# A decoder layer step in split float32 on one core: 30 weight subtractions moved from GpSimd to DVE

## The chip, the cores and the metric

One core of one Trainium2 chip runs the kernel. The metric is the device time of one execution in microseconds, the median over several runs. The engines are TensorE (matmuls; PE and PEld in the profile), DVE (VectorE), ScalarE (ACT), GpSimd (POOL) and SyncE (SP), which here issues most transfers. Each engine works through its own queue in order.

## The reference

One layer of a hybrid decoder, for 1024 prompt tokens and 8 x 4 sample tokens that share all weights (model width 1024). Cut to what matters here:

```python
h = x * (1 + scale1) + shift1
z = h @ w_in                       # q, k, v and the two GLU halves
mix = jnp.concatenate([attn_out, conv_out], axis=-1) @ w_out
x = layer_norm(ALPHA * x + gate1 * mix, ln1_g, ln1_b)
h = x * (1 + scale2) + shift2
up, new_ffn_buf = causal_dwconv(ffn_buf, h @ w_up, ffn_conv_w, ffn_conv_b)   # width 3
up_a, up_b = jnp.split(up, 2, axis=-1)
f = (jax.nn.silu(up_a) * up_b) @ w_down
x = layer_norm(ALPHA * x + gate2 * f, ln2_g, ln2_b)
```

`attn_out` is differential attention, `conv_out` a GLU with a causal convolution of width 31 and a LayerNorm. All arrays are float32.

## The kernel before

**Split products.** Each product of float32 matrices is made of three matmuls in the type float32r: with w = whi + wlo and x = xhi + xlo it adds whi xhi, whi xlo and wlo xhi in PSUM (`mm3`, lines 176 to 178). The high half is a cast, the low half is the float32 value less its high half.

**Tokens and chunks.** The 1056 tokens lie on the free axis in three chunks (`NCH`) of 352 columns (`CH`); the features lie on the partitions in 8 blocks of 128 (`KD`). `gemm8` makes one 128x352 output block with 24 matmuls. A weight block is 128x1024 float32, 512 KB.

**The weight pipeline.** `wsrc` lists the weight blocks in the order of their use, each with the way its low half is made. `prefetch_w` takes the next block: a load by SP into `wst` (2 buffers), a cast on ScalarE into `whi` (L159), and the low half into `wlo` (3 buffers each). The ways are "dma" (ScalarE writes the negated high half, L161, and a DMA of GpSimd's queue adds the original block, L162) or one `tensor_tensor` subtract (L164) on the engine that stands in the list. `next_w` gives out a block and looks two blocks ahead. The load's issue is L303 (`load`).

**The stage around the change.** Behind the attention comes the output projection: for each of the chunks 0, 1, 2 the loop `project` makes 8 output blocks and so takes the 8 blocks of `w_out` once per chunk, 24 in all. DVE adds each block, times its gate, to the residual `acc` (`residual`, L1179). The LayerNorm of chunk 0 is spread over the projection of chunk 1, that of chunk 1 over the projection of chunk 2, and that of chunk 2 over the first FFN group. Its steps (`norm_steps`) are on DVE: a halving sum over the 8 feature blocks (`presum`: L201, then L204 twice, in the tile `bs_s`), then a column sum by TensorE (`colsum`, L210, two for each LayerNorm), the mean taken off (L223), squares by ScalarE (L224), the halving sum again and a second column sum, the reciprocal root (`rstd`: L187 on ScalarE, L189 to L191 on DVE), and its product with the residual (L232). Then `modulate` (L284 to L295, on ScalarE and DVE) makes the high and low halves `h2h` and `h2l` of the FFN's input, and `affine` (L299, GpSimd, 8 steps per chunk) scales the residual.

The FFN works through 11 groups of two feature blocks. The first and the last group (`CHUNK_OUTER`) run their up-products chunk by chunk, and so take their 4 blocks of `w_up` three times each; with the 2 blocks of `w_down` the first group takes 14 blocks. In `Up.chunk` ScalarE takes the product out of PSUM (L1062, L1063), DVE adds the two other taps of the convolution (L1068, L1072) and multiplies the halves (L1079), and GpSimd makes the low half of the result (`al`, L1082); small fills and copies of the state are GpSimd's too (L1048, L1049, L1085, L1086). `down` adds to the residual with L1179.

**Order.** The order of instructions in each engine's queue is drawn up by a list scheduler at compile time; weight loads are kept in program order on SP in the first part of the kernel. Waits are set by the tiles that an instruction reads and writes.

Of the kernel before, what the change touches and what calls it, by code (L numbers as in the profile page):

```python
# [18 lines left out]
KD = D // 128  # L19
# [5 lines left out]
NCH = 3  # L25
# [11 lines left out]
FG = 2  # L37
# [9 lines left out]
CHUNK_OUTER = (0, KF // FG - 1)  # L47
# [21 lines left out]
def body(tc, nc, io):  # L69
    ex = ExitStack()  # L70
    with ex:
# [54 lines left out]
        wsrc = []  # L126
        for w, i in ORDER:
            wsrc += [(io["w_in"][m], "dma") for m in ((16 + i, 12 + i) if w == "g" else (4 * "qkv".index(w) + i, ))]
        wsrc += [(io["w_out"][m], nc.gpsimd) for c in range(NCH) for m in range(KD)]
        for f0 in range(0, KF, FG):  # L130
            once = nc.gpsimd if f0 // FG == CHUNK_OUTER[0] else "dma"

            def blocks(what, how):
                return [(io["w_up"][m], how) for f in range(f0, f0 + FG) for m in (f, KF + f)] if what == "u" else \
                    [(io["w_down"][f], how) for f in range(f0, f0 + FG)]

            if f0 + FG == KF:
                for w, cs in LAST:
                    if w != "n":
                        wsrc += blocks(w, "dma" if len(cs) > 1 else nc.vector)  # L140
            else:
                wsrc += blocks("u", once) * (NCH if f0 // FG in CHUNK_OUTER else 1) + blocks("d", once)
# [1142 lines left out]
```

## Time and profile before

| | us |
|---|---|
| median of 3 runs | 1448.97 |
| lowest and highest run | 1442.78, 1452.08 |
| the profiled execution | 1445.67 |
| its span, first to last instruction | 1443.9 |
| TensorE busy (matmul) | 1354.2 |
| DVE busy | 911.7 |
| ScalarE busy | 643.1 |
| GpSimd busy | 412.9 |

The busy times are of the profiled execution, and are averages over stages that differ: the stage of the change has to be looked at by itself. An instruction that has started and stands because of another engine counts as busy. The granted clock is given as a share of TensorE's full speed of 2.4 GHz, so that 0.50 is the lower level of 1.2 GHz. In the timeline the bracket behind an instruction is the time that its engine was idle before it, and what ended that.

### The profile page before, as it was taken

The page shows a single profiled execution, that of the slowest core. Times are in us where ns is not written, and L with a number is a line of the kernel's source. Part 1 is how long each engine was busy: PE and PEld are TensorE (multiplying, and loading weights), DVE is VectorE, ACT ScalarE, POOL GpSimd, SP SyncE. Part 2 cuts the span into 40 slices and gives each one's busy share as a digit, 9 for nine tenths or more (in the row PEclk, how much of TensorE's full clock was granted, in tenths as well). Part 3 has the DMA queues.
Part 4 walks back from the last instruction along what each step waited for, and adds up shares of the span by engine and source line. Part 5 has one row for each costly group of instructions (what it writes and reads, how often), then busy time and mean ns, then how long its engine had stood idle before and what let it go on. Part 6 is the DMA issues. An engine that isn't in the chain of part 4 may idle for free.

```text
span 1443.9 us, 24578 instructions
## 1 busy us (share of the span) xinstructions
PE 1354.2 (94%) x9449; PEld 1268.2 (88%) x9449; DVE 911.7 (63%) x1924; ACT 643.1 (45%) x1170; POOL 412.9 (29%) x484
## 2 busy tenths in 40 slices
PE   7899999999999898878999999999999999999993
PEld 6798999996766798777999999999999999999983
DVE  5859999427777578897454445454545454536497
ACT  6532222456666554554344343434343434352532
POOL 2431110421110588776121212222222212222111
PEclk9999999999999999989999999999999999999997
DMA  9877666548764254333252434343343434342627
GB/s 311 273 228 199 185 185 191 147 131 288 234 229 172 100 163 143 109 102 102 59 117 65 111 69 108 73 103 81 96 87 90 102 74 100 77 109 67 174 72 207
DMA packets 71670, 199.67 MB, mean 138 GB/s; under 512 B 16002, under 2 KB 16514, under 8 KB 70658
## 3 DMA queue, kind: packets, MB, share of 16 engines
q1 hardware_dynamic: 57874, 145.55, 30.2%
q0 software_dynamic: 13680, 52.57, 18.6%
q8 instruction: 74, 1.21, 0.3%
q14 instruction: 42, 0.34, 0.1%
HBM read 137.49 MB, written 15.51 MB: 106 GB/s over the span
## 4 chain that ended last, share of the span: by engine, by line
PE 70%; DMA 10%; DVE 9%; issue 4%; ACT 4%; POOL 1%; SPq 1%; DVEq 0%; POOLq 0%; ACTq 0%
PE psb L176 20%; PE psb L178 20%; PE psb L177 19%; DMA wlo<-wst 5%; PE psa L836 3%; PE psb L877 2%; DVE t L1068 2%; PE psa L319 1%; PE psb L866 1%; DVE bs_s L204 1%; PE psb L788 1%; PE psb L753 1%; DMA wada<-w_ada 1%; DMA y<-gb 1%; DMA wst<-w_in 1%
## 5 line engine op out<-in xcount | busy, mean ns | idle before, releaser
L1068 DVE SCALAR_TENSOR_TENSOR t<-up,prm,t 128x352 f32<-128x352 f32 (+1 forms) x264 | 177.8, 673 | 288.6 <-ACT t L1063 283.4
L177 PE MATMUL psb<-h2l,whi 128*128 128x352 f32 x1056 | 341.5, 324 | 6.3 <-DVE h2l L295 6.3
L176 PE MATMUL psb<-h2h,whi 128*128 128x352 f32 x1056 | 343.2, 326 | 2.4 <-ACT h2h L294 2.4
L178 PE MATMUL psb<-h2h,wlo 128*128 128x352 f32 x1056 | 339.8, 325 | 0.8 <-DMA wlo<-wst 0.8
L159 ACT CAST whi<-wst 128x1024 fp32r<-128x1024 f32 x124 | 129.2, 1050 | 323.3 <-PE psb L177 278.5
L177 PEld LDWEIGHTS psb<-h2l,whi 128*128 128x128 f32 x1056 | 201.2, 191 | 7.4 <-DVE h2l L295 6.9
L1179 DVE SCALAR_TENSOR_TENSOR acc<-psb,mod,acc 128x352 f32<-128x352 f32 (+1 forms) x288 | 160.3, 571 | 73.0 <-PE psb L178 67.0
L176 PEld LDWEIGHTS psb<-h2h,whi 128*128 128x128 f32 x1056 | 199.8, 189 | 3.0 <-ACT h2h L294 2.7
L178 PEld LDWEIGHTS psb<-h2h,wlo 128*128 128x128 f32 x1056 | 199.6, 190 | 1.9 <-DMA wlo<-wst 1.3
L176 PE MATMUL psb<-ah,whi 128*128 128x352 f32 x528 | 172.1, 328 | 6.5 <-DVE acc L1179 3.3
L178 PE MATMUL psb<-ah,wlo 128*128 128x352 f32 x528 | 166.3, 326 | 8.3 <-DMA wlo<-wst 8.3
L177 PE MATMUL psb<-al,whi 128*128 128x352 f32 x528 | 171.4, 325 | 0.0
L162 POOL DMA_DIRECT2D wlo<-wst x80 | 71.3, 892 | 347.9 <-ACT wlo L161 319.2
L178 PE MATMUL psb<-hh,wlo 128*128 128x352 f32 x480 | 156.8, 327 | 4.3 <-DMA wlo<-wst 4.3
L176 PE MATMUL psb<-hh,whi 128*128 128x352 f32 x480 | 157.8, 335 | 1.5 <-ACT sig L399 1.5
L177 PE MATMUL psb<-hl,whi 128*128 128x352 f32 x480 | 155.8, 325 | 0.0
L375 DVE SCALAR_TENSOR_TENSOR cv<-u,prm,cv 128x1024 f32<-128x1024 f32 x120 | 151.4, 1296 | 0.8
L1082 POOL TENSOR_TENSOR al<-g,ah 128x352 fp32r<-128x352 f32 x60 | 61.3, 1022 | 234.8 <-ACT ah L1080 234.8
L164 POOL TENSOR_TENSOR wlo<-wst,whi 128x1024 fp32r<-128x1024 f32 x38 | 103.5, 2729 | 32.8 <-ACT whi L159 32.7
L176 PEld LDWEIGHTS psb<-ah,whi 128*128 128x128 f32 x528 | 99.7, 189 | 11.1 <-DVE acc L1179 6.4
L178 PEld LDWEIGHTS psb<-ah,wlo 128*128 128x128 f32 x528 | 98.3, 189 | 11.2 <-DMA wlo<-wst 11.2
L177 PEld LDWEIGHTS psb<-al,whi 128*128 128x128 f32 x528 | 99.7, 189 | 0.0
(253 smaller groups left out, 2291.4 us busy)
## 6 DMA issues: line engine op xcount, KB each, us to landing
wlo<-wst POOLq DMA_DIRECT2D x80, 512.0 KB, 5.4
wst<-w_up SPq DMA_DIRECT2D x56, 512.0 KB, 3.7
wada<-w_ada SPq DMA_DIRECT2D x48, 512.0 KB, 5.5
kv<-kc SPq DMA_DIRECT2D x64, 256.0 KB, 5.4
kv<-vc SPq DMA_DIRECT2D x64, 256.0 KB, 4.7
wst<-w_out SPq DMA_DIRECT2D x24, 512.0 KB, 3.7
wst<-w_down SPq DMA_DIRECT2D x24, 512.0 KB, 4.3
wst<-w_in SPq DMA_DIRECT2D x20, 512.0 KB, 3.8
```

The costliest lines, as they stand in the source:

```text
L159: last_w["hi"] = nc.scalar.copy(hi, st)
L162: last_w["lo"] = nc.gpsimd.dma_start(lo.bitcast(F32), st, accum_op=ALU.add)
L164: last_w["lo"] = how.tensor_tensor(lo, st, hi.bitcast(F32), op=ALU.subtract)
L176: nc.tensor.matmul(ps, lhsT=wh, rhs=xh, start=start and i == 0, stop=False)
L177: nc.tensor.matmul(ps, lhsT=wh, rhs=xl, start=False, stop=False)
L178: nc.tensor.matmul(ps, lhsT=wl, rhs=xh, start=False, stop=stop and i == n - 1)
L375: nc.vector.scalar_tensor_tensor(acc, src, wj, acc, op0=ALU.mult, op1=ALU.add)
L836: nc.tensor.matmul(ps[m][:, i, :w], lhsT=q[r], rhs=k[r, i * w:(i + 1) * w], start=True, stop=True)
L877: nc.tensor.matmul(po[:, 0, :128], lhsT=at[:, (kt - k0) * 128:(kt - k0 + 1) * 128], rhs=V[:, kt, h * 128:(h + 1) * 128], start=(kt == 0), ...
L1068: nc.vector.scalar_tensor_tensor(t[:, :npc], up[:, o + j:o + j + npc], w, t[:, :npc], op0=ALU.mult, op1=ALU.add)
L1082: eng.tensor_tensor(self.al[:, c, :], g, self.ah[:, c, :].bitcast(F32), op=ALU.subtract)
L1179: nc.vector.scalar_tensor_tensor(x[:, :npc], ps[:, :npc], gate[:, 0:1], x[:, :npc], op0=ALU.mult, op1=ALU.add)
```

## The change

The subtracts of 30 weight blocks are given to DVE in place of GpSimd: those of `w_out` for chunks 1 and 2 (16), and those of the first FFN group (12 of `w_up`, 2 of `w_down`). The 8 of chunk 0 stay with GpSimd. Nothing else is edited; the scheduler then orders all queues anew.

```diff
-        wsrc += [(io["w_out"][m], nc.gpsimd) for c in range(NCH) for m in range(KD)]
+        wsrc += [(io["w_out"][m], nc.vector if c else nc.gpsimd) for c in range(NCH) for m in range(KD)]
         for f0 in range(0, KF, FG):
-            once = nc.gpsimd if f0 // FG == CHUNK_OUTER[0] else "dma"
+            once = nc.vector if f0 // FG == CHUNK_OUTER[0] else "dma"
```

## Rows read from the trace of the kernel before

**Rows 1.** Busy time by window: stretch, length, busy us per engine, clock, DMA.
```profile
523.00:563.50 40.50, 38.65 (x238) 37.68 (x237) 32.43 (x27) 19.34 (x23) 29.89 (x14) 1.00 0.50 163
563.50:600.60 37.10, 31.05 (x179) 29.50 (x178) 35.28 (x40) 16.10 (x23) 28.43 (x15) 0.95 0.36 108
600.60:677.60 77.00, 59.21 (x318) 55.60 (x316) 68.43 (x91) 45.87 (x78) 62.35 (x57) 0.89 0.31 93
677.60:760.00 82.40, 81.45 (x504) 80.87 (x505) 42.44 (x92) 29.30 (x53) 17.48 (x30) 1.00 0.40 94
```

**Rows 2.** Waits from 523 to 677.6, TensorE's: us in total, times, longest.
```profile
PE psb L210 <- DVE bs_s L204: 14.1, 6, 3.9
PE psb L177 <- DVE h2l L295: 6.3, 2, 4.4
...
PE psb L178 <- POOL wlo L164: 0.4, 1, 0.4
```

**Rows 3.** The line L164, whole span: ns min/median/max, first and last start.
```profile
L164 POOL TENSOR_TENSOR wlo<-wst,whi x38: 2340/2425/4897, 470.2 to 673.0; 128x1024 fp32r<-128x1024 f32 x38
...
L164 DVE TENSOR_TENSOR wlo<-wst,whi x6: 1215/1223/1226, 1367.4 to 1402.0; 128x1024 fp32r<-128x1024 f32 x6
```

**Rows 4.** Timeline of DVE in the stage: start us, us, instruction.
```profile
527.58 2.82 DVE L201 TENSOR_TENSOR bs_s<-acc 128x1408 f32<-128x1408 f32 x1
...
550.97 2.63 DVE L191 SCALAR_TENSOR_TENSOR rs_y<-rs_t,rs_y 128x352 f32<-128x352 f32 x1
...
613.40 1.25 DVE L1068 SCALAR_TENSOR_TENSOR t<-up,prm,t 128x352 f32<-128x352 f32 x2 [2.28 <-POOL up L1048]
...
637.65 0.53 DVE L191 SCALAR_TENSOR_TENSOR rs_y<-rs_t,rs_y 128x352 f32<-128x352 f32 x1
...
674.55 1.13 DVE L1068 SCALAR_TENSOR_TENSOR t<-up,prm,t 128x320 f32<-128x320 f32 x1 [1.51 <-ACT t L1063]
```

**Rows 5.** Timeline of GpSimd in the stage.
```profile
550.82 2.39 POOL L164 TENSOR_TENSOR wlo<-wst,whi 128x1024 fp32r<-128x1024 f32 x1 [2.96 <-ACT whi L159]
...
610.72 2.61 POOL L164 TENSOR_TENSOR wlo<-wst,whi 128x1024 fp32r<-128x1024 f32 x1
```

**Rows 6.** Groups by line and shape on DVE, 523 to 677.6: busy us, mean ns, idle before.
```profile
L232 DVE TENSOR_TENSOR acc<-acc,rs_y 128x2816 f32<-128x2816 f32 x3 | 9.3, 3092 | 0.1
...
L201 DVE TENSOR_TENSOR bs_s<-acc 128x1408 f32<-128x1408 f32 x3 | 8.2, 2729 | 0.1
...
L201 DVE TENSOR_TENSOR bs_s<-sq 128x1408 f32<-128x1408 f32 x3 | 4.9, 1623 | 1.4 <-ACT sq L224 1.3
```

**Rows 7.** Timeline of DVE near the kernel's end, 1360 to 1400.
```profile
1367.38 1.22 DVE L164 TENSOR_TENSOR wlo<-wst,whi 128x1024 fp32r<-128x1024 f32 x1 [1.71 <-ACT whi L159]
...
1394.33 1.22 DVE L164 TENSOR_TENSOR wlo<-wst,whi 128x1024 fp32r<-128x1024 f32 x1
1395.47 0.21 DVE L1117 BATCH_NORM_AGGREGATE nmv<-bn 128x2 f32<-128x12 f32 x1
...
1396.64 1.23 DVE L164 TENSOR_TENSOR wlo<-wst,whi 128x1024 fp32r<-128x1024 f32 x1 [0.25 <-ACT whi L159]
```

**Rows 8.** Waits from 523 to 677.6, those of ScalarE's cast for loads.
```profile
ACT whi L159 <- DMA wst<-w_out: 21.2, 8, 5.2
...
ACT whi L159 <- DMA wst<-w_up: 4.2, 3, 1.9
```

**Rows 9.** Waits from 523 to 677.6 on SP's own queue.
```profile
SPq L303 <- POOL wlo L164: 122.0, 27, 8.5
```

**Rows 10.** Groups by line and shape on GpSimd, 523 to 677.6.
```profile
L299 POOL TENSOR_SCALAR acc<-acc,alph 128x352 f32<-128x352 f32 x24 | 27.8, 1170 | 3.0 <-DVE hf L292 3.0
L1082 POOL TENSOR_TENSOR al<-g,ah 128x352 fp32r<-128x352 f32 x5 | 5.7, 1147 | 4.1 <-ACT ah L1080 4.1
```

**Rows 11.** Busy time by window: four stretches at a lower clock, and their sum.
```profile
586.60:590.10 3.50, 3.19 (x9) 2.71 (x10) 1.93 (x6) 1.50 (x2) 0.06 (x1) 0.51 0.48 150
...
sum 20.60, PE 15.84 PEld 14.21 DVE 15.97 ACT 11.15 POOL 11.87; mean PE 3.96 PEld 3.55 DVE 3.99 ACT 2.79 POOL 2.97
```

## The prediction

> **What bounds the kernel now.** I first cut the span into stretches with the view of busy time by window, because the change touches one stage: its weights are used between 523 and 677.6 us. After it, from 677.6 to 760, TensorE is busy 81.45 of 82.40 us at full clock, so whatever the stage gains or loses reaches the end of the kernel unchanged [rows 1]. I call the stretches A (523 to 563.5: output projection of chunk 1, LayerNorm of chunk 0), B (563.5 to 600.6: projection of chunk 2, LayerNorm of chunk 1) and C (600.6 to 677.6: first FFN group, LayerNorm of chunk 2). In A TensorE is busy 38.65 of 40.50 us and nearly sets the pace. In B and C it is busy 31.05 of 37.10 and 59.21 of 77.00, at clocks of 0.95 and 0.89, while DVE is busy 35.28 and 68.43: there DVE sets the pace [rows 1].
>
> Next, the waits of that stage. TensorE stands 14.1 us before the column sums (L210) for DVE's partial sums, and 6.3 us for DVE's low halves of the FFN input [rows 2]. The LayerNorm chain on DVE is what TensorE's queue waits for.
>
> Then why DVE is so busy. Its timeline has one and the same step in two lengths: L191 at 128x352 takes 0.53 us at 637.65 and 2.63 us at 550.97 [rows 4]. GpSimd began a subtract of 2.39 us at 550.82 [rows 5], and the DVE step ended 0.39 us after it. A DVE step with two SBUF inputs that meets a GpSimd subtract stands until the subtract is over, and this standing is counted as busy. By groups: the halving sum L201, always 128x1408, has a mean of 2729 ns where it reads the residual (two of three beside a subtract) and 1623 ns where it reads the squares [rows 6].
>
> **The change part by part.** 38 subtracts run on GpSimd (median 2425 ns), 6 at the end of the kernel on DVE (1223 ns) [rows 3]. Eight, for chunk 0, stay; 30 move (16 of the projection, 14 of the FFN group).
>
> *Removed from DVE's time: standing.* For each DVE step of the stage I took its duration less that of the same shape undisturbed, and gave the excess to the GpSimd instruction beside it longest. Subtracts account for 24 steps and 42.5 us; the first is L201 at 527.58 (2.82 against 1.62 [rows 6]), the last L1068 at 674.55 [rows 4]. By stretch: A 5 steps, 8.1 us; B 7 steps, 13.2 us; C 12 steps, 21.3 us. In C one more thing goes: DVE idles 2.28 us at 613.40 behind GpSimd's L1048 [rows 4], a small fill that stood in GpSimd's queue behind a subtract of 610.72 to 613.33 [rows 5].
>
> *Added to DVE.* One subtract holds DVE for 1.14 us from its start to the next one's (1394.33 to 1395.47 [rows 7]). One of the 30 falls before 523, where DVE has idle time; A gets 8 (9.1 us), B 8 (9.1), C 13 (14.8).
>
> *Sum by stretch, idle time held as it is.* A: DVE 32.4 - 8.1 + 9.1 = 33.4 of 40.5 us, below TensorE's 38.65: I take 0, with ends of -1.9 (all that TensorE idles) and +1.0 (every subtract on the chain). B: -13.2 + 9.1 = -4.0 (unrounded terms). C: -21.3 + 14.8 - 2.3 = -8.7. Together -12.7 us. What is late next is DVE still: after the change it needs 31.2 of B's 33.1 us and 62.0 of C's 68.3.
>
> *The new wait.* A subtract on DVE waits for ScalarE's cast of the high half (L159), and all LayerNorm steps, products with gate and convolution taps behind it on DVE wait too; TensorE's column sums and FFN input wait for those. GpSimd's queue carried that wait before. The nearest rows are the six DVE subtracts: one stood 1.71 us, when DVE had nothing else, one 0.25 us amid other work, four not at all [rows 7]. Upper end: 1.96 / 6 x 30 = 9.8 us. Lower end below nothing: subtracts depend on no LayerNorm step, so they can fill DVE's idle time, which would take the sum to -22.8 if B and C lost all of theirs (B 31.2 of 37.1, so -5.9; C 62.0 of 77.0, so -15.0) and A its 1.9. I take 0.25 / 6 x 30 = 1.3 us, since the row amid other work is the like one. Result: -11.4 us.
>
> *Loads.* The next weight's load waits on SP's queue for the subtract to release its buffer: 122.0 us in 27 waits [rows 9]. A subtract at 1.14 instead of 2.4 us releases it 1.3 us earlier; a DVE step ahead of it (the longest, L232, is 3.1 us [rows 6]) releases it later. I cost this at nothing because three buffers of each half lie between the subtract and TensorE, which stood for a GpSimd subtract only 0.4 us [rows 2]. If that cover were gone, the price is in the third rival.
>
> *GpSimd.* Without 30 subtracts it still has 24 steps L299 (27.8 us) and 5 low halves L1082 (5.7 us) in the stage [rows 10]. Beside these DVE stands 17 times, 6.1 us in all, and I keep that. The Trainium skill (SBUF — State Buffer, section "SBUF: two separate sides") says that DVE and GpSimd share a port pair as an exclusive lock, and that a DVE step with two SBUF inputs shuts out a GpSimd step that reads SBUF for its whole length: this speaks against the change, since each moved subtract can now hold L299 and L1082. The trace shows the holding in this direction too (L299 at a mean of 1.17 us); by that rule up to 34 us of holding would fall on GpSimd's 33.5 us of work, which fits in 154.6 us, and only the last low half would reach TensorE, +1.1 us on the sum.
>
> **The rivals.**
> 1. *DVE's idle time closes as well.* TensorE's queue has the column sums at fixed places; once DVE no longer slips by 2 us at random points, waits on either side may go. After its longer waits TensorE ran at the lower level of 1.2 GHz: clock 0.51 at 586.6 to 590.1, and three more such stretches, 20.6 us in all [rows 11]. Against it: DVE's need alone fills 31.2 of 37.1 and 62.0 of 77.0 us. Half way from -12.7 to the end of -22.8: -17.8, time 1431 us. The Trainium skill (TensorE: Matmul & The Clock Gate, "HAM oscillation — how this bites in real kernels") describes waits between bursts that slow the next burst; by that rule, waits that go give back up to half of 20.6 us of matmul time, which counts only as far as DVE lets it.
> 2. *Other GpSimd work takes the place of the subtracts.* L299 and L1082 no longer queue behind subtracts and start when their inputs are ready, which is when DVE is at the next step of the same chain. For: they are 33.5 us of work and cost only 6.1 now. Against: the mean L299 is 1.17 us, so one stand is short. If DVE stands for half of it, 16.8 - 6.1 = 10.7 us more: -0.7, time 1448.
> 3. *DVE waits at the head of its queue for the casts; slower.* ScalarE's casts waited 21.2 + 4.2 us for loads in the stage, 11 times [rows 8]. If DVE has its subtract at the head whenever that happens, it stands those 25.4 us: -12.7 + 25.4 = +12.7, time 1462. It decides from a mean stand of 12.7 / 30 = 0.42 us per subtract. Against: rows 7 give 0.04 to 0.33. For: with DVE at 91% in B and C and two load buffers, one late subtract delays the load after next, and the delay returns to DVE.
> 4. *The subtracts don't run as written.* Six of the same kind run on DVE already [rows 3]; I give this nothing.
>
> **How the numbers follow.** The profiled execution took 1445.67 us, 1443.9 of span and 1.8 around it; the median of the three runs is 3.3 above it, and the change of -11.4 is put on the median: 1448.97 - 11.4 = 1437.6. Chances: forecast 0.50 (1433 to 1443), rival 1 0.20, rival 2 0.20, rival 3 0.08, 0.02 for the rest. The range runs from the zero-idle end (1426) to just past rival 2 (1452, which takes in the +9.8 and +1.0 of the unknown costs: 1448.97 - 1.9 = 1447); it leaves out rival 3 and the far tails. A measurement here tells about 1% (14.5 us) from no change. Faster than 1434.5: most of rival 1 and a fifth of the forecast, 0.27. Slower than 1463.5: half of rival 3 and the rest, 0.06. Within: 0.67.
>
> **What the changed profile would show.** 8 GpSimd and 36 DVE subtracts at L164, the latter near 1.22 us. All three L191 at 0.53 us, both kinds of L201 near 1.62. The stage's next full-clock stretch begins some 11 us earlier than 677.6. TensorE's 14.1 us before L210 shrinks to below 8. Wrong if: DVE shows idle time before L164 ended by L159 of more than 12 us (rival 3), excess of DVE steps beside L299 and L1082 of more than 12 us (rival 2), or a granted clock of 1.00 in B and C (rival 1).

## The result and the profile after

| | before | after |
|---|---|---|
| median (us) | 1447.18 (10 runs, 1442.72 to 1455.15) | 1438.88 (10 runs, 1434.58 to 1443.94) |
| ratio | | 0.9946, 95% interval 0.9928 to 0.9965 |
| profiled span (us) | 1443.9 | 1437.3 (run of 1439.02) |

The ratio is a gain of 7.8 us of 1447.18 (5.1 to 10.4 by the interval). The forecast was 11.4. That the forecast time, 1437.6, is so near to the measured 1438.88 is in part luck: it was put on a median of three runs, 1448.97, and that of ten is 1447.18. Two slow runs, of 3110.14 us (e1) and of 1895.21 (e11), are left out of every time and ratio below.

Where the time went is read from three views. First the subtracts and the DVE steps around them, by line and shape from 500 to 680 us (busy us, mean ns, idle before and what ended it):

```profile
L164 DVE TENSOR_TENSOR wlo<-wst,whi 128x1024 fp32r<-128x1024 f32 x30 | 37.1, 1237 | 8.5 <-ACT whi L159 8.5
...
L201 DVE TENSOR_TENSOR bs_s<-sq 128x1408 f32<-128x1408 f32 x3 | 4.9, 1625 | 5.7 <-ACT sq L224 5.7
L201 DVE TENSOR_TENSOR bs_s<-acc 128x1408 f32<-128x1408 f32 x3 | 4.9, 1619 | 0.0
```

Both kinds of L201 now take the same 1.62 us; before, one of them took 2729 ns [rows 6]. The 30 subtracts cost DVE 1237 ns each, near the 1223 of [rows 3]. But DVE now idles 8.5 us behind the casts.

Next, the stretches. These are busy times by window at the same three cuts as [rows 1] (length, PE, PE's weight loads, DVE, ACT, POOL, clock, DMA share, GB/s):

```profile
523.00:563.50 40.50, 38.98 (x241) 38.02 (x240) 34.53 (x38) 20.42 (x25) 5.93 (x6) 1.00 0.54 171
563.50:600.60 37.10, 34.44 (x212) 33.48 (x212) 33.94 (x54) 18.06 (x26) 12.43 (x9) 1.00 0.40 123
600.60:677.60 77.00, 64.02 (x359) 62.01 (x359) 64.32 (x110) 43.17 (x72) 31.53 (x42) 0.89 0.35 101
```

GpSimd's work in A and B fell from 58.3 to 18.4 us. TensorE does 3.4 us more in B and 4.8 more in C: work that used to come later. B is now all at full clock, C is still at 0.89.

Third, what TensorE waits for from 523 to 670, and the timeline of its longest wait:

```profile
PE psb L210 <- DVE bs_s L204: 10.7, 5, 6.5
PE psb L176 <- ACT h2h L294: 3.9, 1, 3.9
PE psb L177 <- DVE h2l L295: 2.5, 1, 2.5
```

```profile
603.75 0.32 PE L178 MATMUL psb<-h2h,wlo 128*128 128x352 f32 x1
610.57 1.51 PE L210 MATMUL psb<-bs_s,ones_d 128*128 128x352 f32 x2 [6.50 <-DVE bs_s L204]
```

The waits for column sums shrank from 14.1 us [rows 2] only to 10.7, and one of them holds 6.5: it is the first column sum of chunk 2's LayerNorm. The same matmul ran at 611.26 in before, so that place moved by less than 1 us on the clock of the trace.

Executions differ by some us ahead of the stage, so I compare positions by their distance from the first matmul of chunk 1's projection (522.88 before, 524.15 after):

| TensorE's place | before | after | change |
|---|---|---|---|
| first column sum, LayerNorm of chunk 1 | 48.6 | 46.7 | -1.9 |
| first matmul of the FFN group | 77.8 | 72.1 | -5.7 |
| first column sum, LayerNorm of chunk 2 | 88.4 | 86.4 | -2.0 |
| second one of it | 107.6 | 101.1 | -6.5 |
| last residual step of the group (DVE L1179) | 174.3 | 161.9 | -12.3 |

From the first matmul of chunk 1's projection to the last of these places, the busy times are (before, then after; columns as above):

```profile
522.88:697.15 174.27, 148.53 (x854) 142.40 (x853) 150.53 (x191) 81.92 (x122) 122.27 (x85) 0.94 0.36 110
524.15:686.09 161.94, 144.79 (x853) 140.84 (x853) 138.47 (x222) 82.36 (x122) 49.89 (x55) 0.95 0.39 118
```

DVE is busy 12.1 us less, and its idle time is the same, 23.7 and 23.5 us: the 8.5 us behind the casts took the place of other idle time.

Not all of the 12.3 us reach the end. Up to the first residual step of the fourth FFN group 2.5 are lost: TensorE waits 3.9 us there for low halves made by DMA, against 2.8 before, and is busy 1.5 us longer with the same matmuls, at a mean granted clock of 0.99 against 1.00. Later 0.4 come back.

From the 261st of the 288 residual steps (L1179, at 1332.90 us in before and 1323.95 after) to the last instruction, both kernels do the same work. It took 111.0 us before and 113.3 after: 2.3 us lost, at the end of the kernel. Up to that step the change is 10.2 us ahead; less the 2.3 lost that is 7.9, and the ratio gives 7.8. The loss shows in TensorE's waits from 1340 to 1440 us, where the last LayerNorm writes out its result (before, then after):

```profile
PE psa L1110 <- DVE y L1131: 3.8, 2, 2.8
```

```profile
PE psa L1110 <- DVE y L1131: 7.7, 2, 4.8
```

DVE's L1131 itself stands there until a buffer of the output y is stored (DVE's waits of the same stretch, 4.4 us in 2 waits before):

```profile
DVE y L1131 <- DMA y<-y: 7.1, 3, 3.6
```

No line of that part was edited. The instruction order differs there, on DVE, ScalarE and the store queue: the scheduler that orders the program drew it anew.

### The profile page after: what moved, and what is told of

The parts are those of the page before. It is cut to its first block, busy times and chain, and to the rows that moved or that the text cites. A ratio compares the mean times of both kernels' runs of the same rounds, so it can differ in the third digit from the quotient of the medians.

```text
span 1437.3 us, 24575 instructions
## 1 busy us (share of the span) xinstructions
PE 1356.3 (94%) x9449; PEld 1271.1 (88%) x9449; DVE 899.7 (63%) x1954; ACT 643.2 (45%) x1170; POOL 338.6 (24%) x454
## 4 chain that ended last, share of the span: by engine, by line
PE 71%; DVE 10%; DMA 9%; issue 5%; ACT 3%; POOL 1%; SPq 0%; DVEq 0%; POOLq 0%; ACTq 0%
PE psb L176 20%; PE psb L178 20%; PE psb L177 19%; DMA wlo<-wst 6%; PE psa L836 4%; PE psb L877 2%; DVE wlo L164 2%; PE psa L319 1%; PE psb L753 1%; PE psb L866 1%; PE psb L788 1%; DMA y<-y 1%; DVE acc L1179 1%; DMA wada<-w_ada 1%; DVE t L1068 1%
## 5 line engine op out<-in xcount | busy, mean ns | idle before, releaser
L1068 DVE SCALAR_TENSOR_TENSOR t<-up,prm,t 128x352 f32<-128x352 f32 (+1 forms) x264 | 165.2, 627 | 282.9 <-ACT t L1063 280.0
L1179 DVE SCALAR_TENSOR_TENSOR acc<-psb,mod,acc 128x352 f32<-128x352 f32 (+1 forms) x288 | 160.4, 571 | 72.6 <-PE psb L178 66.7
L1082 POOL TENSOR_TENSOR al<-g,ah 128x352 fp32r<-128x352 f32 x60 | 60.6, 1010 | 251.8 <-ACT ah L1080 251.8
L1062 ACT COPY up<-psb 128x352 f32<-128x352 f32 (+1 forms) x132 | 58.4, 442 | 88.1 <-PE psb L178 88.0
```

Source lines behind the costliest of these rows:

```text
L1062: nc.scalar.copy(up[:, 2 + o:2 + o + npc], ps[:, 0, :npc])
L1068: nc.vector.scalar_tensor_tensor(t[:, :npc], up[:, o + j:o + j + npc], w, t[:, :npc], op0=ALU.mult, op1=ALU.add)
L1082: eng.tensor_tensor(self.al[:, c, :], g, self.ah[:, c, :].bitcast(F32), op=ALU.subtract)
L1179: nc.vector.scalar_tensor_tensor(x[:, :npc], ps[:, :npc], gate[:, 0:1], x[:, :npc], op0=ALU.mult, op1=ALU.add)
```

## The experiments

In the table, "group" is the shift against before of the last residual step of the first FFN group, and "stage" that of the 261st residual step, each less the shift of the first matmul of chunk 1's projection; "end" is the time from the 261st step to the last instruction (before: 111.0). Negative is earlier. Each comes from one execution of its kernel.

Some expectations below name places by a count that took in, beside the steps, the records of L1179 that only wait, two to five of them in a run. So their "265th residual step" is another step in the change than in before, and with the same step in both, the change's end is 113.3 us and not 114.3. Their 693.3 us for the last residual step of the first group is 697.15 for the same reason.

| kernel | group | stage | end | median (before beside it) | ratio (95%) |
|---|---|---|---|---|---|
| the change | -12.3 | -10.2 | 113.3 | 1438.88 (1447.18) | 0.9946 (0.9928 to 0.9965) |
| e1_out_only | -0.5 | -0.8 | 111.2 | 1447.86 (1446.94) | 0.9998 (0.9975 to 1.0022) |
| e2_ffn_only | -6.4 | -8.1 | 111.8 | 1440.16 (1446.94) | 0.9948 (0.9925 to 0.9970) |
| e3_halves | -2.4 | -2.2 | 110.7 | 1448.24 (1446.94) | 0.9997 (0.9976 to 1.0018) |
| e4_both | +28.5 | +28.4 | 110.5 | 1475.34 (1446.94) | 1.0199 (1.0161 to 1.0237) |
| e5_lock_tt | +9.3 | +9.3 | 111.5 | 1457.99 (1449.32) | 1.0059 (1.0040 to 1.0079) |
| e6_lock_memset | -8.9 | -9.2 | 112.3 | 1443.01 (1449.32) | 0.9962 (0.9943 to 0.9981) |
| e7_dma_ffn | +13.0 | +13.2 | 112.4 | 1463.39 (1449.32) | 1.0106 (1.0086 to 1.0125) |
| e8_one_left | -11.9 | -10.4 | 110.6 | 1436.73 (1449.32) | 0.9927 (0.9905 to 0.9950) |
| e9_colsum_later | -13.5 | -11.2 | 113.0 | 1436.20 (1449.18) | 0.9912 (0.9880 to 0.9944) |
| e10_ln_later | -13.7 | -13.5 | 110.5 | 1433.50 (1449.18) | 0.9891 (0.9861 to 0.9920) |
| e11_al_on_dve | | | | 1434.78 (1449.18) | 0.9904 (0.9872 to 0.9937) |
| e12_all38 | -13.3 | -13.9 | 112.0 | 1432.84 (1449.18) | 0.9896 (0.9862 to 0.9930) |

For e12 both are counted from the first matmul of chunk 0's projection, since its edit reaches back to there. Of e11 only the times are used.

### The two halves of the change alone

e1 moves only the projection's subtracts, e2 only the FFN group's.

```
e1:  wsrc += [(io["w_out"][m], nc.vector if c else nc.gpsimd) ...]   (as in the change)
     once = nc.gpsimd if f0 // FG == CHUNK_OUTER[0] else "dma"       (as before)
e2:  wsrc += [(io["w_out"][m], nc.gpsimd) ...]                       (as before)
     once = nc.vector if f0 // FG == CHUNK_OUTER[0] else "dma"       (as in the change)
```

> Only the 16 subtracts of the projection move to DVE. Theory (the gain is the exchange of DVE's standing behind GpSimd's subtracts for shorter subtracts of its own): DVE's excess beside subtracts of GpSimd is gone from 526 to about 596 us and stays in the FFN group; the first FFN matmul comes about 4 to 6 us earlier than 600.7 us, the median is 3 to 6 us below the kernel before. Rival (the gain comes from the FFN group alone, because TensorE nearly fills the projection): within 1 us of the kernel before at the first FFN matmul.

> Only the 14 subtracts of the first FFN group move. Theory: the first FFN matmul stays at 600 to 601 us, the last residual step of that group's down product comes 5 to 8 us earlier than 693.3 us, the median is 3 to 8 us below the kernel before. Rival (the two parts only work together, since a late projection makes the FFN group late): under 2 us.

e1 gains nothing: its ratio is 0.9998. e2 has the whole of the change's ratio, 0.9948. For e1 the theory held up to the first FFN matmul and failed for the median. Why e1 gains nothing is seen on TensorE and DVE. Its first FFN matmul comes at 594.90, 5.7 us ahead of before's distance, and then TensorE stands at the same column sum of chunk 2:

```profile
602.86 0.32 PE L178 MATMUL psb<-h2h,wlo 128*128 128x352 f32 x1
610.72 1.51 PE L210 MATMUL psb<-bs_s,ones_d 128*128 128x352 f32 x2 [7.55 <-DVE bs_s L204]
```

This is DVE's timeline of e1 ahead of that:

```profile
595.89 0.45 DVE L287 TENSOR_SCALAR hfs<-acc,G,B 128x352 f32<-128x352 f32 x1
...
596.98 2.53 DVE L287 TENSOR_SCALAR hfs<-acc,G,B 128x352 f32<-128x352 f32 x1
...
602.54 3.78 DVE L201 TENSOR_TENSOR bs_s<-acc 128x1408 f32<-128x1408 f32 x1
606.35 1.21 DVE L204 TENSOR_TENSOR bs_s<-bs_s 128x704 f32<-128x704 f32 x1
607.49 2.66 DVE L1068 SCALAR_TENSOR_TENSOR t<-up,prm,t 128x352 f32<-128x352 f32 x1
```

and GpSimd's:

```profile
596.66 2.66 POOL L164 TENSOR_TENSOR wlo<-wst,whi 128x1024 fp32r<-128x1024 f32 x1
...
602.22 2.62 POOL L164 TENSOR_TENSOR wlo<-wst,whi 128x1024 fp32r<-128x1024 f32 x1
...
606.93 2.84 POOL L164 TENSOR_TENSOR wlo<-wst,whi 128x1024 fp32r<-128x1024 f32 x1
```

L287 at 596.98, L201 and L1068 each lie over a subtract of the FFN group that e1 left on GpSimd. DVE works without a gap up to the partial sum that TensorE waits for; arriving there earlier on TensorE only lengthens the wait. In the FFN group of e1 14 DVE steps meet a subtract, with some 24 us of excess, against 12 steps and 21 us before. So a time saved in A and B is kept only if C's DVE work shrinks too. e2 shows the other side. Its first column sum of chunk 2 is 4.8 us later than before's, with the projection's subtracts left on GpSimd as in before; it is 6.4 us ahead by the end of the group and 8.1 by the 261st residual step. By the end of the group the halves alone add up to -6.9 us and together they make -12.3; by the 261st step it is -8.9 and -10.2.

### Shorter subtracts on GpSimd

e3 keeps all 30 on GpSimd, each as two of 128x512.

```
last_w["lo"] = [(nc.gpsimd ...).tensor_tensor(lo[:, j], st[:, j], hi[:, j].bitcast(F32), op=ALU.subtract)
                for j in ((slice(0, 4), slice(4, 8)) if how == "half" else (slice(0, 8),))][-1]
```

> The 30 subtracts stay on GpSimd, each cut in two of 128x512. Theory (a DVE step stands until the GpSimd instruction in progress is over): no stand is longer than about 1.2 us instead of 2.2, the excess of DVE steps beside L164 falls from 42.5 us to 20 to 28, DVE gets no work in return, and the stage ends 8 to 14 us earlier: 1433 to 1440 us. Rival (what counted was that DVE makes the low halves in half the time and so releases the load buffers sooner): GpSimd's work is the same or a little more, so the time is 1446 to 1450 us.

It measured no change (0.9997). The standing only fell from 42.5 to 34.4 us, and came in 42 steps instead of 24: one DVE step gets in between the halves, and the next stands behind the second half. GpSimd's time for the low halves grew as well. By line from 500 to 680 the 60 pieces take 90.8 us, and the five subtracts left whole 12.6; all 35 took 95.8 us before:

```profile
L164 POOL TENSOR_TENSOR wlo<-wst,whi 128x512 fp32r<-128x512 f32 x60 | 90.8, 1535 | 19.6 <-ACT whi L159 19.4 <-PE psb L177 0.2
```

Between the first matmul of chunk 1's projection and the end of the group, DVE was busy 7.7 us less than before (142.8 against 150.5), but idle 5.4 us more (29.1 against 23.7), most of it in front of L1179 for TensorE's products. Why those came late was not followed further. The theory missed both the standing and the time, and the time is the rival's; the rival itself is answered by e5 below.

### Does GpSimd's work make DVE stand, or does DVE's own work count?

e4 gives DVE the subtracts and lets GpSimd repeat each of them in place on the load buffer, where nobody reads it.

```
last_w["lo"] = (nc.vector if how == "both" else how).tensor_tensor(lo, st, hi.bitcast(F32), op=ALU.subtract)
how == "both" and nc.gpsimd.tensor_tensor(st, st, hi.bitcast(F32), op=ALU.subtract)
```

> DVE makes the 30 low halves as in the changed kernel, and GpSimd then repeats each subtract in place on the load buffer, where nobody reads the result. Theory: DVE has its 34 us of subtracts and its standing of 35 to 45 us behind GpSimd as well, so the stage ends 20 to 35 us later than in the kernel before: 1467 to 1482 us. Rival (the gain came from low halves that are there sooner): GpSimd's copy is off every path but the release of the load buffer, so the time stays near the changed kernel's, 1439 to 1447 us.

It is 2% slower, which looks like the standing put back on top of DVE's own work. But the trace names something else as well (TensorE's waits, 523 to 690):

```profile
PE psb L178 <- DVE wlo L164: 16.2, 8, 4.9
PE psb L176 <- ACT whi L159: 8.1, 4, 2.9
```

The repeat holds the load buffer longer and weights come late: TensorE waits 24.3 us for them in a stage that is 28.4 us longer, and waited 0.9 before. The run doesn't separate the two, so I made e5 and e6. Both are e2 with extra work for GpSimd for 12 of the FFN group's 14 blocks, into a scratch tile (one turn of the ring of output buffers) that nothing reads. In e5 it is a subtract, which reads SBUF; in e6 it is two fills, which only write it, with a one-column copy on ScalarE ahead of them.

```
e5:  nc.gpsimd.tensor_tensor(dum[0], hi.bitcast(F32), hi.bitcast(F32), op=ALU.subtract)
e6:  nc.scalar.copy(dum[0][:, 0, 0:1], hi[:, 0, 0:1].bitcast(F32))
     [nc.gpsimd.memset(dum[0], 0.0) for _ in range(2)]
```

> The 14 subtracts of the first FFN group are on DVE as in e2, and for 12 of them GpSimd also subtracts the high half from itself into a scratch tile; no load, low half or matmul waits for that. Theory (DVE stands while a GpSimd instruction that reads SBUF is in progress): 12 instructions of 2.4 us put 12 to 20 us of standing back into the FFN group, TensorE's waits there grow, and the kernel is 8 to 18 us slower than e2, 1448 to 1458 us. Rival (the gain came from earlier low halves and earlier release of the load buffers, which this kernel keeps): 1438 to 1443 us.

> As e5, but GpSimd's extra work is two fills of the same scratch tile each time, which read nothing (a one-column copy by ScalarE ahead of each pair sets their time). Theory: DVE's excess beside these fills stays under 3 us and the time within 3 us of e2, 1437 to 1444 us. Rival (what costs is that GpSimd's queue is full, so that L1082, L299 and the small fills L1048 come late): as slow as e5, 1448 us or more.

This answers the question. With the same DVE work, e5 is slower than before (1.0059) and e6 keeps the gain (0.9962); in the stage they are 18.5 us apart. TensorE waits 18.5 us for column sums in e5 and 13.3 in e6. e5 keeps the low halves and the release of the load buffers on DVE as e6 does (TensorE waits once for one of them, 2.6 us), and yet has lost the gain: so the rival of e3 and e5, that the gain comes from these, fails. One stand of e5, on DVE and on GpSimd:

```profile
633.42 0.88 DVE L204 TENSOR_TENSOR bs_s<-bs_s 128x704 f32<-128x704 f32 x1
634.22 2.21 DVE L1068 SCALAR_TENSOR_TENSOR t<-up,prm,t 128x352 f32<-128x352 f32 x1
636.36 0.51 DVE L204 TENSOR_TENSOR bs_s<-bs_s 128x352 f32<-128x352 f32 x1
636.79 0.57 DVE L1068 SCALAR_TENSOR_TENSOR t<-up,prm,t 128x352 f32<-128x352 f32 x1
```

```profile
633.43 2.62 POOL L164 TENSOR_TENSOR dum<-whi 128x1024 f32<-128x1024 f32 x1 [1.01 <-ACT whi L159]
```

The first L1068 takes 2.21 us and ends 0.38 us after the subtract, the next takes 0.57. In e6, beside two fills in a row, a subtract of DVE and the first of two L1068 keep their times:

```profile
633.53 1.22 DVE L164 TENSOR_TENSOR wlo<-wst,whi 128x1024 fp32r<-128x1024 f32 x1
634.67 1.20 DVE L1068 SCALAR_TENSOR_TENSOR t<-up,prm,t 128x352 f32<-128x352 f32 x2
```

```profile
633.55 1.97 POOL L164 MEMSET dum<- 128x1024 f32 x2 [1.03 <-ACT dum L164]
```

Counted as in the prediction, from 560 to 690 us, the dummy subtracts account for 14 long DVE steps and 19.3 us, the 24 fills for three steps and 0.9 us, each of these with an L299 or L1082 beside it too. The Trainium skill (SBUF — State Buffer, section "SBUF: two separate sides") limits the lock on the shared port pair, for a DVE step with two SBUF inputs, to a GpSimd operation that reads SBUF. The pair e5 and e6 agrees with that: 19.3 us beside readers, at most 0.9 beside writers.

### No DVE and no GpSimd work at all

e7 takes the FFN group's low halves by DMA, as the later groups do; the projection stays as before.

```
once = "dma"
```

> The low halves of the first FFN group are made by the third way: ScalarE writes the negated high half and a DMA of GpSimd's queue adds the block; the projection stays on GpSimd. Neither GpSimd's subtracts nor DVE's are left in the FFN group. Theory (DVE's time sets the pace there): 15 us less DVE work than e2, the stage ends 3 to 8 us earlier than in e2: 1432 to 1438 us. Rival (TensorE's queue, its lower clock and the LayerNorm chain set the pace, not DVE's sum): within 2 us of e2. Third: the DMA's landing of 5.4 us makes low halves late; slower than e2.

1.1% slower, and DVE is not the reason:

```profile
PE psb L178 <- DMA wlo<-wst: 19.5, 12, 3.7
...
PE psb L210 <- DVE bs_s L204: 4.3, 3, 2.5
```

TensorE waits less for column sums than in any other run (4.3 us), but 19.5 us for low halves that land late. The third reading of the expectation came true, so the run doesn't tell what less DVE work alone would give.

### The end, and the fixed places of the column sums

e8 is the change with one projection block (chunk 2, block 3) left on GpSimd, chosen because ScalarE's order and that of the stores at the end of the kernel are those of before there. e9 and e10 are the change with the LayerNorm's steps placed later in TensorE's queue.

```
e8:   nc.vector if c and (c, m) != (2, 3) else nc.gpsimd
e9:   hooks = {0: [steps[2][0]], 2: [steps[2][1]], 3: [steps[2][2]], 4: [steps[2][3], steps[2][4]]}
e10:  hooks = {0: [steps[2][0]], 2: [steps[2][1]], 3: [steps[2][2]], 5: [steps[2][3], steps[2][4]]}
```

> The changed kernel with one projection block (chunk 2, block 3) left to GpSimd: in this kernel the queues of TensorE and ScalarE behind the stage come out in the order of the kernel before. Theory (3 us of the stage's gain are lost at the end because the scheduler drew up the last LayerNorm anew): the stage gains 9 to 12 us as in the changed kernel, the stretch from the 265th residual step to the end is 110 to 111.5 us as in the kernel before (111.0) and not 114.3, the median is 1435 to 1438 us. Rival (the end differs from one execution to the next, whatever the order): 112 us or more again, the median is that of the changed kernel, 1438 to 1440 us.

> The changed kernel with the first column sum of chunk 2's LayerNorm put one output block later into the FFN group (after the third block, not after the second). Theory A (the gain of the projection is lost because the column sum stands at a fixed place in TensorE's queue, ahead of matmuls that could run): TensorE's wait of 6.8 us before that L210 falls under 4 us and the stage ends 2 to 5 us earlier than in the changed kernel; median 1433 to 1437 us. Theory B (DVE's own sum sets the end of the LayerNorm): the wait moves to the later column sum or to the FFN input of chunk 2; TensorE's waits of the FFN group stay at 14 us in all, the stage within 1.5 us.

> As e9, and the last two steps of that LayerNorm also one block later. Theory A: the waits before both L210 fall, 3 to 6 us less than in the changed kernel by the end of the stage. Theory B: the wait for chunk 2's FFN input (4.3 + 3.0 us) grows by what the column sums' waits lose; within 2 us, or later.

e8 has the stage of the change (-10.4 against -10.2), and the end is back at 110.6; its wait there is that of before again:

```profile
PE psa L1110 <- DVE y L1131: 3.9, 2, 2.9
```

Over all kernels this wait before L1110 goes with the order in which SP's queue stores y. It is 3.8 to 3.9 us in the seven traced kernels with the order of before (before, e1, e3, e4, e8, e10, e12), and 7.4 to 7.7 in the six others, in which a store of L1141 goes ahead of the last one of L1143, the two lines that store y (the change, e2, e5, e6, e7, e9; in e2, e7 and e9 a part of it stands as a wait for DVE's L1121). So the longer wait goes with the order, without an exception. The time of the end follows it less closely: 110.5 to 112.0 us in the seven, 111.5 to 113.3 in the six. What else moves it was not followed.

e9 shows that the 6.5 us of wait are not the fault of the place alone: with the first column sum later, the wait moved to the second one (7.1 us, its longest), TensorE's waits of the group stay at 12.5 us (12.9 in the change), and the group ends 1.2 us earlier, which is theory B. Moving both (e10) spreads it (TensorE's waits, 523 to 690):

```profile
PE psb L210 <- DVE bs_s L204: 10.3, 6, 3.3
```

The group ends 1.4 us earlier than in the change, less than theory A asked for, and the wait for the FFN input did not grow as theory B had it. By the 261st step e10 is 3.3 us ahead of the change, since it loses less in the next two groups (0.8 us instead of 2.5), and the end is back at 110.5. Stage and end together are 6.2 us; the medians, 1438.88 and 1433.50, differ by 5.4.

### Taking more off GpSimd

e11 is the change with the low halves L1082 of the first group on DVE as well, e12 the change with the eight subtracts of chunk 0's projection on DVE as well.

```
e11:  eng = nc.vector if self.f >= KF - FG or self.f < FG else nc.gpsimd
e12:  wsrc += [(io["w_out"][m], nc.vector) for c in range(NCH) for m in range(KD)]
```

> The changed kernel with the 6 low halves L1082 of the first FFN group on DVE as well. They are 0.52 us each on DVE where the last group has them, so 3.1 us of DVE work for 3.2 us of standing beside L1082. Theory (exchange of standing for work, nothing gained when both are equal): the stage within 2 us of the changed kernel's. Its queues of TensorE and ScalarE at the end come out as in the kernel before: the stretch from the 265th residual step to the end 109.5 to 111.5 us, the median 1435 to 1438 us. If the end's order doesn't matter: 112 us or more.

> All 38 subtracts on DVE. Theory: chunk 0's 8 subtracts cost DVE 9.1 us where it has idle time and save it 5 us of standing; the projection gives its gain back at the column sum as in e1, so the FFN group starts earlier or equal and the stage ends as in the changed kernel within 2 us. Its queues of TensorE and ScalarE at the end too come out as in the kernel before: 109.5 to 111.5 us for the end, the median 1435 to 1438 us.

Both beat the kernel before by 1%. e12's group ends 1.0 us ahead of the change's, as forecast, and its stage 3.7; its end, 112.0 us, is above the forecast 109.5 to 111.5. e12 is the fastest kernel measured, at 1432.84 us. Its interval (0.9862 to 0.9930) overlaps the change's (0.9928 to 0.9965) only at the edge, so that it also beats the change is likely rather than shown. e10's interval lies below the change's, but the two were measured on different runs of the kernel before.

## Why the prediction was right, and where not

1. *The standing goes.* Right. None of the 24 long steps is left in the stage; ahead of it, at 520.93, one L986 stands 1.5 us beside a subtract of chunk 0. That a GpSimd subtract, which reads SBUF, makes DVE stand, and a fill, which only writes it, does not, is shown by e5 against e6.
2. *A subtract costs DVE 1.14 us.* Right: the 30 have a mean duration of 1237 ns, against the 1223 of the rows from which 1.14 was taken. Over the whole span 36 are on DVE and 8 on GpSimd, as forecast.
3. *The sum by stretch, A 0, B -4.0, C -8.7.* The total held and the shares did not. TensorE was 1.9 us ahead by the column sum of chunk 1, which is A's far end, 5.7 by the first FFN matmul, 2.0 by the next column sum and 12.3 by the end of the group. The step that failed is that each stretch's gain is kept: two thirds of the 5.7 are gone 14 us later, where TensorE's queue meets a DVE chain without slack, and come back only as C's own DVE work shrinks. e1 shows the part of A and B to be worth next to nothing alone (-0.5 by the end of the group), e2 shows C's to be worth 6.4 alone.
4. *The new wait, +1.3.* Mis-sized as a wait, near in what it cost: it is 8.5 us of idle time, 0.28 us for each of 30, inside the upper end of 9.8 and short of the 0.42 at which rival 3 decides. The mean of the six rows, 0.33, was nearer than the one stand amid other work, from which I took 0.04. But DVE's idle time from the first matmul to the end of the group is 23.7 us before and 23.5 after, so other idle time went in its place, and the sum came out at -12.3 all the same. That this would happen I had argued only for the lower end of the range, so in this term the sum was helped by luck. DVE's busy time fell by 12.1 us, a little more than the 9.5 that 42.5 of standing less 33.0 of subtracts gives.
5. *Loads at nothing.* Right: TensorE has no wait for a low half in the stage, and SP's queue stood 118.7 us in 28 waits for DVE's subtracts, against 122.0 in 27 [rows 9].
6. *Other GpSimd work, 6.1 us kept.* Nearly right: DVE's long steps beside L299 and L1082 came to 7.6 us (4.5 and 3.1), far from rival 2's 16.8. The hold in the other direction was small too: L299's mean went from 1170 ns [rows 10] to 1371, which is 4.8 us over 24 steps and not 34.
7. *Rival 1, idle time closes as well.* It did not: DVE's idle time stayed. In B the clock rose from 0.95 to 1.00, but in C it stayed at 0.89, and the waits for column sums came to 10.7 us, not below the 8 that I had named.
8. *Whatever the stage gains reaches the end.* This failed, by 4.4 us of 12.3. I had read that TensorE is busy after 677.6 and took the rest of the kernel as fixed. But 2.1 are gone by the 261st residual step, through waits for low halves made by DMA and a lower clock in the two groups behind, and 2.3 more at the end, where the instruction order is another one.

So -11.4 was near for the stage (-12.3 by the end of the group), and the kernel's -7.8 is that less what the rest of the kernel lost.

## What to carry to other kernels

When one and the same DVE step shows two lengths, look at what GpSimd does beside the long ones: the excess is time that DVE gets back if that work goes to another place, and what it is worth is read where TensorE's queue next waits for DVE, not where the step stands. Do each half of such a change alone; here one half alone was worth nothing, and the other, by the ratio, as much as both. When you compare places in two traces, make sure that you count the same instruction in both. Where a scheduler orders the whole program, compare the instruction order and the time of the stages that were not edited as well: 4.4 of 12.3 us were lost there.

## What the runs showed of the hardware that I had not expected

- DVE also stands in L287, which has a single large input and per-partition factors: 2.53 us at 596.98 in e1, beside a GpSimd subtract, against 0.45 us at 595.89, beside an L299. I had spoken only of steps with two inputs.
- Halving the GpSimd instruction hardly cuts the standing: 42.5 us in 24 steps became 34.4 in 42 (e3).
- A fill of 128x1024 on GpSimd, about 0.98 us each in the row above, leaves DVE alone although it writes as much SBUF as a subtract.
